# FFN and gate of a four-layer decoder trunk as one piece in a fixed order, fed by one stream of weights

## The chip, the cores and the metric

The kernel runs on one core of a Trainium2 chip. The metric is the device time of one execution in microseconds (us). The engines are called as the profile calls them: PE (TensorE's matmuls; PEld its weight loads), DVE (VectorE), ACT (ScalarE), POOL (GpSimd) and SP (SyncE, which issues all DMAs here).

## The reference, cut to what matters

Four layers; each adds a token mixer, a SwiGLU FFN and a gated embedding to a residual stream `h` of 256 tokens by 1024. The mixers are latent attention (layers 0 and 3), a Conformer convolution (layer 1) and an HGRN2 recurrence (layer 2). All is float32.

```python
for i in range(DEPTH):                       # 4
    u = _rmsnorm(h, norm1_g[i])
    h = h + mixer_i(u)                       # mla, conv, hgrn2, mla
    h = h + _swiglu(_rmsnorm(h, norm2_g[i]), ffn_w_gu[i], ffn_w_down[i])   # 1024 -> 2 x 2816 -> 1024
    gate = jax.nn.sigmoid(_rmsnorm(h, ple_norm_g[i]) @ ple_w_gate[i])      # 1024 -> 1024
    h = h + (p[i] @ ple_w_proj[i]) * gate
return _rmsnorm(h, final_norm_g)
```

## The kernel before, in words

**Matmuls.** The 256 tokens are two tiles of 128 (t = 0, 1). Every float32 operand is split into a high and a low float32r part, and `mm` (lines 219 to 224) makes three matmuls for each product: high x high, high x low, low x high. The token operand is the stationary side; the weights move, 512 columns at a time.

**Weights.** `granule` (168 to 189) loads 512 KB of weights into a buffer `raw` (4 buffers) and splits it: ACT copies the high part (`whi`, 9 buffers, line 182), then DVE subtracts for the low part (`wlo`, 8 buffers, line 183). Only when DVE is done is that `raw` free for the next load. `ktiles` (191) makes granules of two k-tiles of 128 rows by 512 columns; a gate-up granule has two DMAs, the others one. `behind()` orders a split after the instructions in `T.fence`.

**The token side.** `Norm.do(t)` (66 to 89) squares `h` on ACT (line 74, two halves of 512 columns), forms the reciprocal root with eleven small DVE instructions that hang on each other (`rsqrt`, 270 to 294), and transposes 8 blocks of 128 on PE in two groups of four (`split_T`, line 257). Each block leaves PSUM as a high part by ACT (264) and a low part by DVE (265). A `full` norm (before conv and hgrn) first writes `hg` = `h` times the root (line 83, DVE, two halves); the others transpose `h` itself and use the root later. With `defer` (before hgrn) tile 1 is transposed only after the first projection of tile 0 (`finish`, 91).

**FFN** (`ffn`, 359 to 415). Eleven column blocks j of 256. For each (j, t): `up`, 24 matmuls (8 k-tiles x 3) into a bank of gate and up columns; ACT makes Silu (`sg`, 376), DVE the product `ga` (378); two transposes and a split give `aT` (244, 245); `down`, 12 matmuls, adds into four PSUM banks that live through all j. The transposes of a step are put behind the second k-tile of the next `up` (`between`). At the end `residual` (353) adds to `h` and the gate's norm follows. `conv_setup` (layer 0) and `hgrn_setup` (layer 1) are called at j = 2: constants for the mixers of the next layers, a small load `lg`, one transpose of it, an Exp on ACT and about thirty small DVE instructions.

**Gate** (`gate`, 459 to 475, through `linear`, 306). Four groups (t, c) of 24 matmuls, c a half of the 1024 columns; `use` (468 to 473) takes each group with a Tanh on ACT (471) and two DVE instructions (472, 473). After (0, 1) the next norm's tile 0 is done, after (1, 0) the first weights of the next mixer are loaded and split (`pre`), after (1, 1) tile 1.

**What sets the order.** The framework places instructions on each engine by its own estimate of when they are ready, in the order of the program where several are; it may move an instruction of the FFN past another. The engines then run their lists in order. Only the inside of `conv` has an order written by hand: `in_order` (205) chains all instructions of an engine made within it. The 12 small matmuls of `idle` (435) in conv, which have no use but to keep PE at work, go wherever the framework finds a hole.

Of the kernel before, what the change touches and what calls it, by code (L numbers as in the profile page):

```python
# [57 lines left out]
class Norm:  # L58
# [3 lines left out]
    def __init__(self, T, name, i, full=False, defer=False):  # L62
        self.T, self.g, self.full, self.defer = T, T.gains(name, i), full, defer
        self.x, self.r = None, [None] * NT

    def do(self, t):
        T, nc = self.T, self.T.nc
        if self.x is None:
            self.x = T.operand(KD)
        h = T.h[t]  # L70
        ss = T.tmp("ss", [P, 2], 4)
        halves = [slice(c * 512, (c + 1) * 512) for c in range(2)]
        for c, s in enumerate(halves):
            square = nc.scalar.activation(T.tmp("junk", [P, 512], 1, BF16), h[:, s], AF.Square, accum_out=ss[:, c : c + 1])
        if not self.full:
            fence = T.split_T(h, self.x, 0, t, self.g)
        tot = T.tmp("sst", [P, 1], 4)
        nc.vector.tensor_tensor(out=tot, in0=ss[:, 0:1], in1=ss[:, 1:2], op=ALU.add)
        r = self.r[t] = T.rsqrt(tot, 1.0 / D)
        if self.full:  # L80
            hg = T.tmp("hg", [P, D], 1)
            for s in halves:
                last = nc.vector.tensor_scalar(out=hg[:, s], in0=h[:, s], scalar1=r, scalar2=None, op0=ALU.mult)
            if t == NT - 1 and self.defer:
                self.hg = hg
                fence = [square.ins, last.ins]
            else:
                fence = T.split_T(hg, self.x, 0, t, self.g)
        T.fence = fence

    def finish(self, behind):

        with self.T.tc.issue_after(behind):
            self.T.fence = self.T.split_T(self.hg, self.x, 0, NT - 1, self.g)


class Out:


    def __init__(self, T, row):  # L100
        self.T, self.g = T, T.gain(row)

    def do(self, t):
        T, nc = self.T, self.T.nc
        h = T.h[t]
        ss = T.tmp("ss", [P, 2], 4)
        halves = [slice(c * 512, (c + 1) * 512) for c in range(2)]
        for c, s in enumerate(halves):
            nc.scalar.activation(T.tmp("junk", [P, 512], 1, BF16), h[:, s], AF.Square, accum_out=ss[:, c : c + 1])
        tot = T.tmp("sst", [P, 1], 4)  # L110
        nc.vector.tensor_tensor(out=tot, in0=ss[:, 0:1], in1=ss[:, 1:2], op=ALU.add)
        r = T.rsqrt(tot, 1.0 / D)
        y = T.tmp("hg", [P, D], 1)
        for s in halves:
            nc.vector.scalar_tensor_tensor(out=y[:, s], in0=h[:, s], scalar=r, in1=self.g[:, s], op0=ALU.mult, op1=ALU.mult)
            nc.sync.dma_start(T.out[t * P : (t + 1) * P, s], y[:, s])


class Trunk:
# [235 lines left out]

    def ffn_head(self, i):
        return self.ktiles(self.a["ffn_w_gu"][i], [(0, 256), (DFF, 256)])

    def ffn(self, i, norm, done, pre):
        nc = self.nc  # L360
        wgu, wdn = self.a["ffn_w_gu"][i], self.a["ffn_w_down"][i]
        NJ = DFF // 256
        with self.scope(self.nm("ffn")) as pool:
            acc = [[self.acc() for c in range(2)] for t in range(NT)]
            ws, aT = {0: self.head}, {}

            def up(j, t, between=None):
                if t == 0:
                    if j:
                        ws[j] = self.ktiles(wgu, [(j * 256, 256), (DFF + j * 256, 256)])  # L370
                    aT[j] = self.operand(2, "aT", 6, pool)
                r = norm.r[t]
                ps = self.bank("mm", 2)
                self.mms(ps, self.cut(norm.x, t), ws[j], between)
                sg = self.tmp("sg", [P, 256], 2, pool=pool)
                nc.scalar.activation(sg, ps[:, :256], AF.Silu, scale=r)  # L376
                ga = self.tmp("ga", [P, 256], 2, pool=pool)
                nc.vector.scalar_tensor_tensor(out=ga, in0=ps[:, 256:], scalar=r, in1=sg, op0=ALU.mult, op1=ALU.mult)  # L378
                return lambda: self.split_T(ga, aT[j], 0, t)

            wd = {}

            def down(j, t):
                if t == 0:
                    wd[j] = [self.granule([(wdn[(2 * j + k) * P : (2 * j + k + 1) * P], 0)], 1, D) for k in range(2)]
# [6 lines left out]
                if j == NJ - 1:  # L392
                    for c in range(2):
                        self.residual(t, c, acc[t][c])
                    done(t)

            turn = None
            for j in range(NJ):
                if j == 2 and i == 0:
# [4 lines left out]
                if j:  # L404
                    down(j - 1, 1)
                if j == NJ - 1:
                    turn()
                    down(j, 0)
# [796 lines left out]
```

## Time and profile before

| | us |
|---|---|
| median of 3 runs | 1404.83 |
| lowest, highest | 1404.08, 1407.93 |
| the profiled execution's own time | 1409.67 |
| its span, first to last instruction | 1407.9 |

The profiled execution took 1.77 us more than its span, and 4.84 us more than the median of the runs. Times within it count from its first instruction. The mean granted clock is 0.99. Matmul records carry a modelled end, so the distance from one start to the next is read rather than the length of a record. A few matmul records are missing.

### The profile page before, as it was taken

The page shows a single profiled execution, that of the slowest core. Times are in us where ns is not written, and L with a number is a line of the kernel's source. Part 1 is how long each engine was busy: PE and PEld are TensorE (multiplying, and loading weights), DVE is VectorE, ACT ScalarE, POOL GpSimd, SP SyncE. Part 2 cuts the span into 40 slices and gives each one's busy share as a digit, 9 for nine tenths or more (in the row PEclk, how much of TensorE's full clock was granted, in tenths as well). Part 3 has the DMA queues.
Part 4 walks back from the last instruction along what each step waited for, and adds up shares of the span by engine and source line. Part 5 has one row for each costly group of instructions (what it writes and reads, how often), then busy time and mean ns, then how long its engine had stood idle before and what let it go on. Part 6 is the DMA issues. An engine that isn't in the chain of part 4 may idle for free.

```text
span 1407.9 us, 20128 instructions
## 1 busy us (share of the span) xinstructions
PE 1349.1 (96%) x7153; PEld 1100.0 (78%) x7153; DVE 898.1 (64%) x1855; ACT 750.0 (53%) x1353; POOL 14.6 (1%) x51
## 2 busy tenths in 40 slices
PE   6899999999898999999899999999999899999997
PEld 6677788787886888887788887878878777788875
DVE  6866555548787855556777768555568856655546
ACT  6776544436535654445654536444447766544444
POOL 0000000000000000000000000000000000000000
PEclk9999999999999999999999999999999999999999
DMA  6512655553685565554474434655543512766532
GB/s 201 183 61 90 209 182 184 184 169 112 225 241 166 162 211 182 180 179 141 128 224 135 128 91 139 220 179 180 181 159 121 195 60 78 226 191 194 190 109 90
DMA packets 174021, 228.14 MB, mean 162 GB/s; under 512 B 11712, under 2 KB 138848, under 8 KB 173920
## 3 DMA queue, kind: packets, MB, share of 16 engines
q1 hardware_dynamic: 173920, 226.85, 51.1%
q8 instruction: 56, 0.92, 0.3%
q14 instruction: 45, 0.37, 0.1%
HBM read 222.27 MB, written 1.05 MB: 159 GB/s over the span
## 4 chain that ended last, share of the span: by engine, by line
PE 67%; DVE 12%; DMA 9%; ACT 9%; issue 3%; SPq 1%; DVEq 0%; ACTq 0%
PE mm L222 12%; PE mm L224 12%; PE mm L223 12%; PE acc L223 7%; PE acc L224 7%; PE acc L222 7%; DVE wlo L183 4%; ACT whi L182 4%; PE tr L257 3%; DMA raw<-in_ffn_w_down_dram 2%; DVE xT L265 2%; DMA raw<-in_ffn_w_gu_dram 1%; ACT xT L264 1%; DMA raw<-in_ple_w_gate_dram 1%; PE acc L1057 1%
## 5 line engine op out<-in xcount | busy, mean ns | idle before, releaser
L183 DVE TENSOR_TENSOR wlo<-raw,whi 128x1024 fp32r<-128x1024 f32 (+2 forms) x420 | 496.3, 1199 | 169.1 <-ACT whi L182 124.0
L182 ACT ACTIVATE whi<-raw 128x1024 fp32r<-128x1024 f32 (+2 forms) x420 | 428.9, 1041 | 242.0 <-DMA raw<-in_ffn_w_down_dram 87.3
L222 PE MATMUL mm<-whi,xT 128*128 128x512 f32 x816 | 328.8, 403 | 0.0
L223 PE MATMUL mm<-wlo,xT 128*128 128x512 f32 x816 | 320.9, 393 | 1.7 <-DVE wlo L183 1.7
L224 PE MATMUL mm<-whi,xT 128*128 128x512 f32 x816 | 322.0, 395 | 0.0
L224 PEld LDWEIGHTS mm<-whi,xT 128*128 128x128 f32 x816 | 153.5, 188 | 32.5
L223 PEld LDWEIGHTS mm<-wlo,xT 128*128 128x128 f32 x816 | 154.0, 189 | 31.7 <-DVE wlo L183 2.7
L222 PEld LDWEIGHTS mm<-whi,xT 128*128 128x128 f32 x816 | 153.9, 189 | 29.3 <-ACT xT L264 0.4
L223 PE MATMUL acc<-wlo,aT 128*128 128x512 f32 x352 | 138.6, 394 | 0.0
L222 PE MATMUL acc<-whi,aT 128*128 128x512 f32 x352 | 138.5, 394 | 0.0
L224 PE MATMUL acc<-whi,aT 128*128 128x512 f32 x352 | 136.2, 389 | 0.1
L378 DVE SCALAR_TENSOR_TENSOR ga<-mm,rs_y,sg 128x256 f32<-128x256 f32 x88 | 42.3, 480 | 139.8 <-ACT sg L376 139.8
L376 ACT ACTIVATE sg<-mm,rs_y 128x256 f32<-128x256 f32 x88 | 40.9, 465 | 134.6 <-PE mm L224 134.5
L222 PE MATMUL acc<-whi,xT 128*128 128x512 f32 (+2 forms) x272 | 103.4, 385 | 5.4 <-ACT xT L264 4.4
L223 PE MATMUL acc<-wlo,xT 128*128 128x512 f32 (+2 forms) x272 | 104.1, 384 | 2.8 <-DVE wlo L183 2.8
L224 PE MATMUL acc<-whi,xT 128*128 128x512 f32 (+2 forms) x272 | 103.3, 382 | 0.3 <-DVE xT L265 0.3
L264 ACT ACTIVATE xT<-tr,gT 128x128 fp32r<-128x128 f32 x208 | 68.2, 363 | 41.4 <-PE tr L257 21.0
L222 PEld LDWEIGHTS acc<-whi,aT 128*128 128x128 f32 x352 | 66.1, 188 | 16.4 <-ACT aT L244 2.0
L224 PEld LDWEIGHTS acc<-whi,aT 128*128 128x128 f32 x352 | 66.1, 188 | 15.9 <-DVE aT L245 1.2
L223 PEld LDWEIGHTS acc<-wlo,aT 128*128 128x128 f32 x352 | 66.2, 188 | 13.0
L265 DVE SCALAR_TENSOR_TENSOR xT<-tr,gT,xT 128x128 fp32r<-128x128 f32 x208 | 67.0, 345 | 12.1 <-ACT xT L264 9.0
L245 DVE TENSOR_TENSOR aT<-tr,aT 128x256 fp32r<-128x256 f32 x88 | 37.2, 423 | 54.1 <-ACT aT L244 54.1
(266 smaller groups left out, 1759.9 us busy)
## 6 DMA issues: line engine op xcount, KB each, us to landing
raw<-in_ffn_w_gu_dram SPq DMA_DIRECT2D x352, 256.0 KB, 4.4
raw<-in_ffn_w_down_dram SPq DMA_DIRECT2D x88, 512.0 KB, 4.5
raw<-in_ple_w_gate_dram SPq DMA_DIRECT2D x32, 512.0 KB, 4.9
raw<-in_hgrn_w_in_dram SPq DMA_DIRECT2D x64, 256.0 KB, 4.1
raw<-in_mla_w_out_dram SPq DMA_DIRECT2D x16, 512.0 KB, 4.0
raw<-in_conv_w_pw_dram SPq DMA_DIRECT2D x32, 256.0 KB, 4.6
raw<-in_mla_w_in_dram SPq DMA_DIRECT2D x16, 336.0 KB, 3.4
raw<-in_mla_w_uq_dram SPq DMA_DIRECT2D x12, 384.0 KB, 3.8
```

Of the source, the lines that this page charges most:

```text
L182: nc.scalar.activation(hi[:, :used], raw[:, :used], AF.Copy)
L183: nc.vector.tensor_tensor(out=lo[:, :used], in0=raw[:, :used], in1=hi[:, :used].bitcast(F32), op=ALU.subtract)
L222: mm(ps, x[0], w[0], start=start, stop=False)
L223: mm(ps, x[0], w[1], start=False, stop=False)
L224: return mm(ps, x[1], w[0], start=False, stop=stop)
L245: v = self.nc.vector.tensor_tensor(out=lo, in0=src, in1=hi.bitcast(F32), op=ALU.subtract)
L257: nc.tensor.transpose(pt[:, (i - k0) * P : (i - k0 + 1) * P], src[:, i * P : (i + 1) * P], self.ident)
L264: a = nc.scalar.activation(hi, pv[:, i - k0], AF.Copy, scale=g[i])
L265: v = nc.vector.scalar_tensor_tensor(out=lo, in0=pv[:, i - k0], scalar=g[i], in1=hi.bitcast(F32), op0=ALU.mult, op1=ALU.subtract)
L376: nc.scalar.activation(sg, ps[:, :256], AF.Silu, scale=r)
L378: nc.vector.scalar_tensor_tensor(out=ga, in0=ps[:, 256:], scalar=r, in1=sg, op0=ALU.mult, op1=ALU.mult)
L1057: nc.tensor.matmul(ps[:, hh, t], kb[:, hh, tok(t)], right(qf[:, hh, tok(t)]), start=True, stop=True)
```

## The change

`ffn` and `gate` become one function inside `in_order(PE, ACT, DVE, SP)`: the instructions of each of these four engines run as the program lists them. The order is written out: in each step `up` of two k-tiles, the transposes of the step before, weight splits (two `down` granules at t = 0; three granules of the next block at t = 1, the fourth after the Silu), the other six k-tiles, the Silu and product, `down` of the step before. The last block, the gate, the residuals, the two norms around the gate and the next mixer's first splits follow in a written order with three endings (`close`): before conv, hgrn and mla; the fourth, `store`, is the final norm, which took the place of the class `Out`.

All weights of an FFN, its gate and the beginning of the next mixer come from one `Stream`: a list of granules in the order of their use. Four are loaded when the stream is made (in the mixer's `pre`), and each split is followed by the load of the granule four further on. `Norm.do` is cut into `squares`, `root` and `turn`. `hgrn_setup` and `conv_setup` are now called inside the order, behind step (2, 1). The number of matmuls, splits, norms and bytes stays as it was. `lg` is loaded on SP's list where `hgrn_setup` stands in the order.

The core of the diff (mixers take their first weights from the stream instead of from `conv_head` and the like; that is left out):

```diff
+class Stream:
+    AHEAD = 4
+    def __init__(self, items):
+        self.items, self.loaded = list(items), []
+        for _ in range(self.AHEAD):
+            self.load()
+    def load(self):
+        if self.items:
+            later = []
+            self.loaded.append((self.items.pop(0)(later), later))
+    def split(self, n=1):
+        out = []
+        for _ in range(n):
+            x, later = self.loaded.pop(0)
+            for f in later:
+                f()
+            self.load()
+            out.append(x)
+        return out
...
+        items = [row(0), row(1)]
+        for j in range(1, DFF // 256):
+            items += self.granules(wgu, [(j * 256, 256), (DFF + j * 256, 256)])
+            items += [row(2 * j), row(2 * j + 1)]
+        for c in range(2):
+            items += self.granules(wg, [(c * 512, 512)])
+        self.stream = Stream(items + self.mixer_items(i + 1))
+        return head
...
+        with self.scope(self.nm("ffn")) as pool, self.in_order(ENG.PE, ENG.Activation, ENG.DVE, ENG.SP):
...
+            steps = [(j, t) for j in range(NJ) for t in range(NT)]
+            for n, (j, t) in enumerate(steps[:-1]):
+                last = steps[n - 1] if n else None
+                up(j, t, 0, 2)
+                if last:
+                    turn(*last)
+                if t == 0:
+                    wd[j] = w.split(2)
+                elif j + 1 < NJ:
+                    ws[j + 1] = sum(w.split(3), [])
+                up(j, t, 2, KD)
+                act(j, t)
+                if t == 1 and j + 1 < NJ:
+                    ws[j + 1] += w.split(1)[0]
+                if last:
+                    down(*last)
+                if j == 2 and t == 1 and i == 0:
                     self.conv_setup()
-                if j == 2 and i == 1:
+                if j == 2 and t == 1 and i == 1:
                     self.hgrn_setup()
-                turn = up(j, 0, turn)
-                if j:
-                    down(j - 1, 1)
-                if j == NJ - 1:
-                    turn()
-                    down(j, 0)
-                    turn = up(j, 1)
-                    pre()
-                    turn()
-                else:
-                    turn = up(j, 1, turn)
-                    down(j, 0)
-            down(NJ - 1, 1)
-
-
-    def embed_weights(self, i, later=None):
+            j = NJ - 1
+            turn(j, 0)
+            up(j, 1, 0, 2)
+            gate_weights(0, 2)
+            down(j, 0)
+            for c in range(2):
+                self.residual(0, c, acc[0][c])
+            gnorm.squares(0)
+            up(j, 1, 2, 5)
+            gnorm.turn(0, 0)
+            up(j, 1, 5, 6)
+            gnorm.turn(0, 1)
+            up(j, 1, 6, KD)
+            act(j, 1)
+            gate_weights(0, 2)
+            gnorm.root(0)
+            gate(0, 0, 0, 3)
+            turn(j, 1)
+            gate(0, 0, 3, KD)
+            gate_weights(1, 2)
+            use(0, 0)
+            down(j, 1)
+            for c in range(2):
+                self.residual(1, c, acc[1][c])
+            gnorm.squares(1)
+            gate_weights(1, 2)
+            gate(0, 1, 0, 3)
+            gnorm.turn(1, 0)
+            gate(0, 1, 3, 6)
+            gnorm.turn(1, 1)
+            gate(0, 1, 6, KD)
+            gnorm.root(1)
+            use(0, 1)
+            self.close(i, nnorm, gate, use, w)
...
+    def close(self, i, nnorm, gate, use, w):
+        gate(1, 0, 0, KD)
+        if nnorm is None:
+            self.store(gate, use)
+            return
+        kind = (i + 1) % 3
+        nnorm.squares(0)
+        nnorm.root(0)
+        if kind == 1:
+            w.split(1)
+            use(1, 0)
+            self.wp = w.split(1)
+            gate(1, 1, 0, 4)
+            nnorm.turn(0, 0)
+            gate(1, 1, 4, KD)
+            nnorm.turn(0, 1)
+            self.wp += w.split(1)
+        elif kind == 2:
+            use(1, 0)
+            gate(1, 1, 0, 2)
+            nnorm.turn(0, 0)
+            head = w.split(1)[0]
+            gate(1, 1, 2, KD)
+            nnorm.turn(0, 1)
+            head += w.split(1)[0]
+        else:
+            use(1, 0)
+            gate(1, 1, 0, 2)
+            nnorm.turn(0, 0)
+            head = w.split(1)
+            gate(1, 1, 2, KD)
+            nnorm.turn(0, 1)
+            head += w.split(1)
+        use(1, 1)
+        nnorm.squares(1)
+        if kind == 0:
+            nnorm.turn(1, 0)
+            head += w.split(2)
+            nnorm.turn(1, 1)
+            nnorm.root(1)
+            head += w.split(4)
+        else:
+            nnorm.root(1)
+            if kind == 1:
+                head = w.split(2)
+                head = head[0] + head[1]
+                nnorm.turn(1)
+            else:
+                head += w.split(1)[0] + w.split(1)[0]
+        self.head = head
```

`store` runs, after `gate(1, 0)`: the squares of tile 0, its root, scaling and output, `use(1, 0)`, the first square of tile 1, `gate(1, 1)`, `use(1, 1)`, the second square, root, scaling and output of tile 1.

More of the change, by code (lines that the diff above doesn't have):

```diff
@@ L91, in finish @@
     def finish(self, behind):
         with self.T.tc.issue_after(behind):
[L94 to L116, printed above, removed]
+            self.turn(NT - 1)
```

227 lines of the change are left out of this document (135 added, 92 removed).

## The prediction

> **What bounds the kernel now.** I read the page first, for the shares.
>
> ```profile
> span 1407.9 us, 20128 instructions
> PE 1349.1 (96%) x7153; PEld 1100.0 (78%) x7153; DVE 898.1 (64%) x1855; ACT 750.0 (53%) x1353; POOL 14.6 (1%) x51
> ```
>
> PE is the bound over the whole, so a change of order can gain only what PE still waits. Next I cut the span into stretches: from a layer's first FFN matmul to the last matmul of its gate (four rows), then from there to the end of the next mixer's first projections (24 narrow conv matmuls; 48 of hgrn; 96 of mla) or to the end (four rows). Columns: stretch, its length, busy time and count of PE, PEld, DVE, ACT, POOL, granted clock, DMA.
>
> ```profile
> 134.76:351.88 217.12, 214.46 (x972) 172.79 (x970) 126.02 (x206) 107.88 (x168) 2.83 (x9) 1.00 0.55 175
> 474.49:689.20 214.71, 213.08 (x964) 172.63 (x963) 126.33 (x218) 109.84 (x170) 0.00 (x0) 1.00 0.56 178
> 857.15:1073.86 216.71, 213.99 (x966) 172.52 (x965) 131.29 (x212) 112.83 (x174) 0.00 (x0) 1.00 0.57 180
> 1184.31:1398.00 213.69, 211.46 (x955) 171.70 (x953) 124.17 (x199) 105.00 (x160) 0.00 (x0) 1.00 0.54 174
> ...
> 351.88:369.10 17.22, 13.18 (x56) 10.13 (x57) 13.83 (x31) 12.61 (x23) 2.36 (x1) 0.87 0.82 277
> 689.20:706.50 17.30, 14.16 (x58) 10.84 (x57) 14.22 (x30) 12.30 (x21) 0.00 (x0) 0.90 0.51 135
> 1073.86:1091.00 17.14, 16.50 (x109) 15.65 (x108) 13.41 (x54) 12.62 (x32) 0.29 (x1) 1.00 0.45 144
> 1398.00:1407.90 9.90, 0.17 (x1) 0.00 (x0) 4.59 (x15) 1.41 (x3) 0.00 (x0) 0.72 0.14 53
> ```
>
> The four FFN and gate stretches are 862.2 us together, and PE is idle in only 9.2 of them. The pitch of the matmuls gives the rest of what can be lost: from the PE timeline, start to start.
>
> ```profile
> 201.97 0.40 PE L224 MATMUL mm<-whi,xT 128*128 128x512 f32 x1
> 202.20 0.38 PE L257 MATMUL tr<-ident,ga 128*128 128x128 f32 x2
> 202.66 0.40 PE L223 MATMUL mm<-wlo,xT 128*128 128x512 f32 x1
> ...
> 203.13 0.39 PE L222 MATMUL mm<-whi,xT 128*128 128x512 f32 x1
> ...
> 206.32 0.39 PE L224 MATMUL mm<-whi,xT 128*128 128x512 f32 x1
> ...
> 692.74 0.39 PE L222 MATMUL mm<-whi,xT 128*128 128x512 f32 x1
> ...
> 695.23 0.39 PE L224 MATMUL mm<-whi,xT 128*128 128x512 f32 x1
> 698.26 1.14 PE L257 MATMUL tr<-ident,hg 128*128 128x128 f32 x8 [2.65 <-DVE hg L83]
> ...
> 699.97 0.63 PE L223 MATMUL mm<-wlo,xT 128*128 128x512 f32 x1
> ...
> 702.53 0.43 PE L223 MATMUL mm<-wlo,xT 128*128 128x512 f32 x1
> ```
>
> From 203.13 to 206.32 there are 14 steps, from 692.74 to 695.23 eleven: 0.228 and 0.226 us, so 0.227. Two transposes add (202.66 - 201.97) - 2 x 0.227 = 0.236, or 0.118 each. A stretch holds 22 x 36 + 96 = 888 matmuls and 72 transposes (64 in the last): 201.6 + 8.5 = 210.1 us (209.1). So the four lose 862.2 - 839.4 = 22.8 us. That is all the FFN and gate have to give. The waits of PE say to whom:
>
> ```profile
> PE tr L257 <- DVE hg L83: 6.1, 4, 2.6
> PE tr L257 <- DVE ga L378: 3.3, 6, 1.5
> PE acc L223 <- DVE wlo L183: 2.8, 5, 0.7
> PE mm L223 <- DVE wlo L183: 1.7, 3, 0.7
> ```
>
> Every one is DVE. So I looked for what DVE must do around the gate: mean durations between 312 and 372 us, and one reciprocal root alone on DVE.
>
> ```profile
> L183 DVE TENSOR_TENSOR wlo<-raw,whi 128x1024 fp32r<-128x1024 f32 x16 | 18.9, 1219 | 2.9 <-ACT whi L182 2.9
> L182 ACT ACTIVATE whi<-raw 128x1024 fp32r<-128x1024 f32 x16 | 16.1, 1050 | 3.5 <-DMA raw<-in_ple_w_gate_dram 2.5 <-DMA raw<-in_conv_w_pw_dram 1.0
> L74 ACT ACTIVATE junk<-h 128x512 bf16<-128x512 f32 x8 | 5.0, 629 | 5.3 <-DVE h L353 3.1 <-DVE h L473 2.2
> L353 DVE TENSOR_TENSOR h<-acc,h 128x512 f32<-128x512 f32 x4 | 2.7, 687 | 2.0 <-PE acc L224 2.0
> L473 DVE TENSOR_TENSOR h<-h,th 128x512 f32<-128x512 f32 x4 | 2.7, 684 | 0.0
> ...
> 358.35 0.16 DVE L78 TENSOR_TENSOR sst<-ss 128x1 f32<-128x1 f32 x1 [0.17 <-ACT junk L74]
> ...
> 360.25 0.16 DVE L292 SCALAR_TENSOR_TENSOR rs_y<-rs_t,rs_y 128x1 f32<-128x1 f32 x1
> 360.45 0.88 DVE L83 TENSOR_SCALAR hg<-h,rs_y 128x512 f32<-128x512 f32 x2
> ```
>
> A low part takes 18.9/16 = 1.18 us of DVE, a residual or gate addition 0.69, a root alone 2.06 (358.35 to 360.41), `hg` 0.9. A block of a norm's transposes (high by ACT, low by DVE) takes 0.39 in a row of them, since ACT waits for DVE again after each pair:
>
> ```profile
> 362.79 0.62 ACT L264 ACTIVATE xT<-tr,gT 128x128 fp32r<-128x128 f32 x2 [0.49 <-PE tr L257]
> ...
> 365.14 0.37 ACT L264 ACTIVATE xT<-tr,gT 128x128 fp32r<-128x128 f32 x1 [0.16 <-DVE xT L265]
> ```
>
> (six steps in 2.35 us). A group of four is 1.6.
>
> **The change part by part.**
>
> ```profile
> L378 DVE SCALAR_TENSOR_TENSOR ga<-mm,rs_y,sg 128x256 f32<-128x256 f32 x88 | 42.3, 480 | 139.8 <-ACT sg L376 139.8
> L376 ACT ACTIVATE sg<-mm,rs_y 128x256 f32<-128x256 f32 x88 | 40.9, 465 | 134.6 <-PE mm L224 134.5
> ```
>
> *FFN steps.* A step is 36 matmuls and two transposes, 8.4 us, with three splits on average, 3.5 us of DVE and 3.2 of ACT, and Silu and `ga` at 0.5 each. Loads go out about a step before their split. A `ga` is wanted 18 matmuls (4.1 us) after its `up`, 6 (1.4) in the first step, and its chain is 1.2. So the waits for `ga` and for `wlo` into `mm` go, at most 5.0 us of idle, and nothing in the steps is late next.
>
> *The gate block, where `up(10,1)` ends (time 0).* DVE's list in the new order, each end by the sums above: four blocks of the second transposes and `ga` 1.6; two low parts 4.0; root 6.0; `aT` 6.4; two low parts 8.8; the two instructions of `use(0,0)` 10.3 with its halved root; two residuals 11.7. Then ACT: last square with its read-out 12.5, high part 13.5. DVE: low part 14.7. That low part is wanted by k-tile 4 of `gate(0,1)`. PE gets there after 9 + 15 + 12 + 9 + 3 matmuls and 6 transposes, 10.9 + 0.7 = 11.6. So PE loses 3.1 us here, at several points (`aT`, residual, whole weights), because behind one late instruction the fixed order holds all others of its engine: residuals stand behind four splits and a root that nobody wants yet. A wait costs its restart too: from 695.23 to 698.26 are 3.03 us for 2.65 idle and one pitch, 0.15 more; at five points 0.8. That is 3.9 a layer, 15.6 for four, and about 1 more in layer 1, where the transposes before hgrn wait for `hg`: 16.6. Against 22.8 now: -6. But of the 22.8, 9.2 are idle and some 5 restarts and the small matmuls that fill holes; some 8 no row names, and if those stay it is +2. I take -3, nearer to the first, as most small losses stand beside waits. If all the idle time went it would be -9.
>
> *`hgrn_setup`.* Its DMA has been on its way for 45 us when it is wanted. Rows of the `lg` tile and of the DMA issues:
>
> ```profile
> L954 SPq DMA_DIRECT2D lg<-in_hgrn_lb_logits_dram x1: 347/347/347, 461.4 to 461.4; - x1
> L956 PE MATMUL tr<-ident,lg x1: 244/244/244, 506.3 to 506.3; 32*128 32x32 f32 x1
> ...
> DMA to landing us min/median/max: 1.5/1.5/1.5
> ```
>
> In the new order it stands on SP behind a load whose `raw` comes free when DVE has done the fourth split of the step: Silu, high part, low part, 0.5 + 1.05 + 1.22 and lags, 3.1 us after `up(2,1)`; then two issues and its own at 0.35, landing 1.5: 5.7. The transpose of it is next on PE after `down(2,0)`, 12 matmuls, 2.7. Wait 3.0 us. What is queued behind: on PE `up(3,0)`, on ACT the Exp and the splits, on DVE some thirty small ones. They delay `aT` of (2,1), which PE wants 7 us later, so no second wait; POOL, 1% busy, has its part done before. `conv_setup` has two loads and no reader in the FFN: 0. At the rows above, a wait of 2.65 us is followed by a pitch of 0.427 (699.97 to 702.53, six steps), 1.8 us lost until the pitch is back. So 3.0 + 1.8 = 4.8, between 2 and 5. TensorE: Matmul & The Clock Gate of the Trainium skill, in its part on oscillation, has the clock fall only after idle gaps above some 3.4 us; by that this term would be 3.0. The trace shows the fall after 2.65, and I go by the trace.
>
> *The endings.* Here `turn(0,1)` and a split stand ahead of the last Tanh, and everything after it hangs on that. First DVE's lag when the last gate matmul ends. From the end of `gate(0,1)`: transposes' blocks and root 3.9, `use(0,1)` 5.4, square 6.2, root 8.2, `hg` 9.1, embedding input 9.8, `use(1,0)` 11.3, low part 12.5, four blocks 14.0; PE needs 48 matmuls and four transposes, 11.4. DVE lags 2.6 (before hgrn, without the input and with PE itself waiting, 1.0; before mla, without `hg`, 0.8).
> Conv: after the last gate matmul 0.45 transposes, 1.6 blocks, 1.2 low part, 1.4 `use`, 0.8 square, 2.1 root, 0.9 `hg`, 2.4 two low parts, 0.7 first block, and the lag: 13.9 to the first matmul, 5.9 more for the other blocks and the last two low parts: 19.8, and 1.2 at the lower clock: 21.0. Now 17.2: +3.8. The 24 matmuls of the embedding (5.5 us) lie within.
> Hgrn: the third granule's low part comes after 0.45 + 1.6 + 1.2 + 1.4 + 0.8 + 2.1 + 0.9 + 1.2 + 1.0 = 10.6; 12 matmuls 2.7, transposes 0.9, 24 matmuls 5.4, lower clock 1.8: 21.4. Now 17.3: +4.1. Its cover, 24 matmuls for tile 0, is gone with the two granules that are split last.
> Mla: granules are 672 columns, low part 1.18 x 672/1024 = 0.8. The fifth comes after 0.45 + 1.6 + 0.8 + 1.4 + 0.8 + 1.6 + 1.6 + 1.6 + 2.1 + 0.8 + 0.8 = 13.5; the work of the last four of eight granules on both tiles, half of 16.5 - 13 x 0.118, is 7.5: 21.0. Now 17.1: +3.9, and +0.5 if PE finds tile 1's work to fill with.
> The final norm: the chain after the last gate matmul is the same: 0.
>
> Sum: -3 + 4.8 + 3.8 + 4.1 + 3.9 = +13.6 us. On the profiled execution, 1409.67 us for a span of 1407.9, that makes 1423.3; on the median of 1404.83, which is 4.84 us lower, 1418.4.
>
> **The rivals.**
>
> *The order covers.* If DVE's list in the gate block is done by 11.6 instead of 14.7, and the endings cost what they cost now, the 9.2 us of idle time go: 1395.6, faster. It decides where one root and one split (2.06 + 1.18) of DVE's list find room in its pauses, so that nothing stands behind them. For it: DVE is busy 58% of these stretches (507.8 of 862.2). Against it: the written order has the roots in one piece.
>
> *Nothing measurable.* The lists come out close to what the framework made, and gains in the steps (5.0) are given back at `lg` (4.8): 1404.6, with the endings as they are. Against it: the endings are written anew.
>
> *The clock falls in every gate block too.* Then 4 x 1.8 us more: 1425.6. Against it: there each wait is near 1 us.
>
> **How the numbers follow.** The forecast has a chance of 0.51, the first rival 0.30, the second 0.13, the third 0.06. Within 0.3% (4.2 us, about what a measurement of this kernel can tell) is the second: 0.13; faster 0.30; slower 0.57. The range reaches from the first rival to the third, 1395 to 1426. The forecast's own range is 1410 (endings and `lg` at half their price) to 1425.
>
> **What would show it.** In the changed profile: in the FFN steps no wait of PE for `ga`; a wait of about 3 us for the transpose of `lg`; waits for residual and `wlo` near the gate, 3 us a layer; a stretch of some 21 us behind each of three gates, with DVE busy throughout. Wrong it would be if DVE has idle time between `up(10,1)` and the next mixer while PE runs on, or if those stretches stay at 17 us.

## The result, and the profile after

The changed kernel takes 1489.12 us (median of four runs, 1487.12 to 1491.3); the kernel before, on the same chip, 1406.38 (1404.08 to 1412.26). The ratio is 1.058, 95% interval 1.0545 to 1.0619. Slower was forecast, by 13.6 us; it is slower by 83, far outside the range.

The head of the page after, then the same eight stretches as before, with the same columns: four from a layer's first FFN matmul to its last gate matmul, four from there to the end of the mixer's first projections or of the program.

```profile
span 1489.5 us, 19835 instructions
PE 1384.3 (93%) x7153; PEld 1116.1 (75%) x7153; DVE 911.3 (61%) x1855; ACT 739.6 (50%) x1353; POOL 15.9 (1%) x51
```

```profile
136.70:359.50 222.80, 216.81 (x973) 173.87 (x972) 124.64 (x197) 103.03 (x159) 3.16 (x9) 1.00 0.55 172
492.60:724.50 231.90, 220.21 (x962) 176.04 (x961) 129.34 (x226) 104.10 (x163) 0.00 (x0) 0.98 0.52 165
903.60:1131.90 228.30, 219.92 (x961) 176.19 (x959) 128.49 (x203) 105.29 (x164) 0.00 (x0) 0.98 0.54 168
1253.60:1479.70 226.10, 219.15 (x955) 175.52 (x953) 125.82 (x199) 101.97 (x158) 0.00 (x0) 0.98 0.52 167
```

```profile
359.50:388.33 28.83, 17.06 (x61) 12.36 (x60) 20.77 (x41) 16.73 (x32) 3.10 (x1) 0.73 0.46 148
724.50:750.76 26.26, 17.71 (x63) 12.01 (x62) 15.38 (x35) 15.12 (x29) 0.00 (x0) 0.81 0.29 82
1131.90:1157.42 25.52, 20.70 (x116) 17.94 (x115) 17.20 (x47) 15.91 (x40) 0.00 (x0) 0.93 0.41 130
1479.70:1489.50 9.80, 0.00 (x0) 0.00 (x0) 4.62 (x15) 1.53 (x5) 0.00 (x0) 0.62 0.14 54
```

The four FFN and gate stretches are 909.1 us together against 862.2 (+46.9); PE is idle in 33.0 of them, not 9.2. From a layer's last gate matmul to the next layer's first FFN matmul (359.5 to 492.6, 724.5 to 903.6, 1131.9 to 1253.6) it is 433.9 against 401.0: +32.9, of which 29.0 lie in the three stretches of the endings above and the rest in the mixers. The first FFN begins 1.9 us later, and the end is what it was. PE's longest waits are for ScalarE and VectorE; the load of `lg` is one wait of 5.2:

```profile
PE acc L244 <- ACT whi L204: 13.8, 9, 4.1
PE tr L279 <- DVE ga L431: 12.3, 8, 3.1
PE acc L245 <- DVE wlo L205: 7.6, 12, 1.7
...
PE tr L1127 <- DMA lg<-in_hgrn_lb_logits_dram: 5.2, 1, 5.2
```

But both are busy for a smaller share than before. So what did they wait for? The groups of the blocks of `xT` say it. First before, then after (columns: busy and mean, then the engine's idle time just ahead of them and what ended it):

```profile
L264 ACT ACTIVATE xT<-tr,gT 128x128 fp32r<-128x128 f32 x208 | 68.2, 363 | 41.4 <-PE tr L257 21.0 <-DVE xT L265 19.1
L265 DVE SCALAR_TENSOR_TENSOR xT<-tr,gT,xT 128x128 fp32r<-128x128 f32 x208 | 67.0, 345 | 12.1 <-ACT xT L264 9.0
```

```profile
L286 ACT ACTIVATE xT<-tr,gT 128x128 fp32r<-128x128 f32 x208 | 71.5, 365 | 69.9 <-DVE xT L287 56.7 <-PE tr L279 12.7
L287 DVE SCALAR_TENSOR_TENSOR xT<-tr,gT,xT 128x128 fp32r<-128x128 f32 x208 | 69.4, 348 | 56.5 <-ACT xT L286 54.9
```

The blocks last as long as ever, but each engine now waits for the other: ScalarE 56.7 us in place of 19.1, VectorE 54.9 in place of 9.0. One turn of the third layer's gate norm, on ScalarE:

```profile
1115.74 0.37 ACT L286 ACTIVATE xT<-tr,gT 128x128 fp32r<-128x128 f32 x1 [1.49 <-DVE xT L287]
1116.53 0.37 ACT L286 ACTIVATE xT<-tr,gT 128x128 fp32r<-128x128 f32 x1 [0.42 <-DVE xT L287]
1117.31 0.81 ACT L286 ACTIVATE xT<-tr,gT 128x128 fp32r<-128x128 f32 x2 [0.42 <-DVE xT L287]
1118.54 0.37 ACT L286 ACTIVATE xT<-tr,gT 128x128 fp32r<-128x128 f32 x1 [0.42 <-DVE xT L287]
```

A block starts every 0.79 us, each behind VectorE's low part of the block before; only once do two follow at once, where the turn goes over from one PSUM bank to the other. In both traces a block on ScalarE waits on VectorE's semaphore until the low part of the block before it in the same bank is done. Before, the framework had mixed the blocks of a turn's two banks, so that the block just ahead lay in the other bank and a pair of blocks waited 0.16 us (the prediction's rows from 362.79 to 365.14). The change fixes four from one bank, then four from the other, so that the block just ahead lies in the same bank and each block waits 0.42 us. The Trainium skill (PSUM — Partial Sum Buffer, the section on bank collisions) gives the reason: two engines must not touch a bank, in the same partitions, at the same time, reads against reads included, and the compiler's scheduler puts a dependency between them. The waits here agree with it; what happens without them was not tried.

The theory to be tested: this pairing is the largest part of the loss. Its rival: the places of the splits, residuals and Tanh in the fixed lists are.

### The profile page after: what moved, and what is told of

It is laid out like the page before. It is cut to its first block, busy times and chain, and to the rows that moved or that the text cites. A ratio compares the mean times of both kernels' runs of the same rounds, so it can differ in the third digit from the quotient of the medians.

```text
span 1489.5 us, 19835 instructions
## 1 busy us (share of the span) xinstructions
PE 1384.3 (93%) x7153; PEld 1116.1 (75%) x7153; DVE 911.3 (61%) x1855; ACT 739.6 (50%) x1353; POOL 15.9 (1%) x51
## 4 chain that ended last, share of the span: by engine, by line
PE 73%; DVE 12%; ACT 9%; issue 3%; DMA 2%; SPq 0%; ACTq 0%; DVEq 0%
PE mm L244 13%; PE mm L245 13%; PE mm L246 13%; PE acc L245 8%; PE acc L246 8%; PE acc L244 8%; DVE wlo L205 4%; DVE xT L287 3%; ACT whi L204 3%; ACT xT L286 2%; PE tr L279 2%; PE acc L1228 1%; PE acc L849 1%; PE tr L831 1%; DVE rs_t L309 1%
## 5 line engine op out<-in xcount | busy, mean ns | idle before, releaser
L205 DVE TENSOR_TENSOR wlo<-raw,whi 128x1024 fp32r<-128x1024 f32 (+2 forms) x420 | 491.1, 1205 | 105.3 <-ACT whi L204 94.2
L204 ACT ACTIVATE whi<-raw 128x1024 fp32r<-128x1024 f32 (+2 forms) x420 | 417.4, 1036 | 52.3 <-PE mm L246 20.0
L244 PE MATMUL mm<-whi,xT 128*128 128x512 f32 x816 | 335.6, 412 | 4.5 <-ACT whi L204 2.9
L245 PE MATMUL mm<-wlo,xT 128*128 128x512 f32 x816 | 326.9, 401 | 4.5 <-DVE wlo L205 4.5
L246 PE MATMUL mm<-whi,xT 128*128 128x512 f32 x816 | 326.0, 400 | 0.0
L244 PEld LDWEIGHTS mm<-whi,xT 128*128 128x128 f32 x816 | 155.8, 191 | 37.6 <-ACT whi L204 4.3
L246 PEld LDWEIGHTS mm<-whi,xT 128*128 128x128 f32 x816 | 155.5, 191 | 36.0
L266 ACT ACTIVATE aT<-tr 128x256 fp32r<-128x256 f32 x88 | 33.8, 384 | 271.4 <-PE tr L279 271.4
L244 PE MATMUL acc<-whi,xT 128*128 128x512 f32 (+2 forms) x272 | 107.0, 403 | 13.9 <-ACT whi L204 7.3
L245 PE MATMUL acc<-wlo,xT 128*128 128x512 f32 (+2 forms) x272 | 107.6, 398 | 6.5 <-DVE wlo L205 6.5
L246 PE MATMUL acc<-whi,xT 128*128 128x512 f32 (+2 forms) x272 | 106.4, 394 | 0.3 <-DVE xT L287 0.3
L286 ACT ACTIVATE xT<-tr,gT 128x128 fp32r<-128x128 f32 x208 | 71.5, 365 | 69.9 <-DVE xT L287 56.7
L287 DVE SCALAR_TENSOR_TENSOR xT<-tr,gT,xT 128x128 fp32r<-128x128 f32 x208 | 69.4, 348 | 56.5 <-ACT xT L286 54.9
L246 PEld LDWEIGHTS acc<-whi,aT 128*128 128x128 f32 x352 | 66.1, 188 | 17.2 <-DVE aT L267 2.6
```

What stands on the lines that cost most here:

```text
L204: nc.scalar.activation(hi[:, :used], raw[:, :used], AF.Copy)
L205: nc.vector.tensor_tensor(out=lo[:, :used], in0=raw[:, :used], in1=hi[:, :used].bitcast(F32), op=ALU.subtract)
L244: mm(ps, x[0], w[0], start=start, stop=False)
L245: mm(ps, x[0], w[1], start=False, stop=False)
L246: return mm(ps, x[1], w[0], start=False, stop=stop)
L266: a = self.nc.scalar.activation(hi, src, AF.Copy)
```

## The experiments

Unless an interval is given, a time is of one run. The runs were made in groups, each on a chip of its own, with the kernel before beside it: 1407.95 (`e1`, `e2`, `e4`, `e5`), 1411.40 (`e3`, `e6`, `e7`, `e8`), 1406.66 (`e9` to `e12`), 1406.23 (`f1`, `g1` to `g3`) and 1410.69 (`g4`). Most differences below are between groups, and the kernel before itself lay between 1402 and 1412, so differences under some 5 us are read from the profiles.

**The banks, in the kernel after.** `e1_alternate`:

```diff
 def turn(self, t, half=None):
...
+        if half == 1:
+            return
-        T.fence = T.split_T(src[:, k0 * P : k1 * P], self.x, k0, t, self.g[k0:k1])
+        T.fence = T.split_T(src, self.x, 0, t, self.g)
 def split_T(self, src, x, k, t, g=None):
...
+            blocks += [(i, pv[:, i - k0]) for i in range(k0, k1)]
+        if blocks and self.pinned:
+            blocks.sort(key=lambda b: (b[0] % 4, b[0] // 4))
+        for i, pb in blocks:
```

> Edit of the kernel after: each turn of a norm inside the pinned piece turns all eight parts at once, into both transpose banks, and its eight blocks are split in the order A0, B0, A1, B1, ..., instead of four from one bank and then four from the other. Bank theory (a block on ScalarE waits for VectorE's read of the block before it in the same PSUM bank, so a block takes 0.79 us where two banks in turn take 0.39, and ScalarE and VectorE arrive late at everything queued behind): the wait of xT on ScalarE for xT on VectorE falls from 56.7 us to about 20 (19.1 before the change), and the time falls by 30 to 50 us, to about 1440 to 1460. Rival, order theory (what costs is where the weight splits, the tanh and the residuals stand in the fixed lists; the blocks are only what these lists wait beside): the xT wait falls as well, but the time stays within 8 us of 1489.

`e2_bank_order` is the same with `key=lambda b: b[0]`.

> The control to the run before: the same turning of all eight parts at once, but the blocks split bank by bank (A0 to A3, then B0 to B3), as the kernel after has them. Bank theory: nothing of the loss comes back, 1489 within 8 us, and the xT wait stays at 50 to 60 us. Rival (the early transposes are what helps, since PE has them out of its way): the same gain as the run before.

Measured: 1455.12 and 1488.89. On ScalarE, `e1_alternate` (a turn takes the blocks in quick pairs) and the row of its group:

```profile
1097.14 0.62 ACT L292 ACTIVATE xT<-tr,gT 128x128 fp32r<-128x128 f32 x2 [1.23 <-DVE xT L293]
1097.93 0.62 ACT L292 ACTIVATE xT<-tr,gT 128x128 fp32r<-128x128 f32 x2 [0.16 <-DVE xT L293]
1098.72 0.63 ACT L292 ACTIVATE xT<-tr,gT 128x128 fp32r<-128x128 f32 x2 [0.16 <-DVE xT L293]
```

```profile
L292 ACT ACTIVATE xT<-tr,gT 128x128 fp32r<-128x128 f32 x208 | 68.2, 364 | 40.7 <-DVE xT L293 25.8 <-PE tr L282 13.2
```

and of `e2_bank_order`:

```profile
L292 ACT ACTIVATE xT<-tr,gT 128x128 fp32r<-128x128 f32 x208 | 71.0, 365 | 67.6 <-DVE xT L293 54.6 <-PE tr L282 12.6
```

Two blocks every 0.79 us, 0.39 each. ScalarE's wait falls to 25.8 us, not quite to 20. The two kernels differ in nothing but the order of 104 blocks (13 turns inside the piece), and in 33.8 us. The early transposes give nothing. This part is shown: 34 of 83 us. How much of it are the waits themselves, and how much the lower clock behind them, was not taken apart.

**The banks, in the kernel before.** `e5_before_bank_order` holds only the blocks of those turns in bank order (`pin` is set for the gate's norms and the first norms of layers 1 to 3; the deferred turn before hgrn goes by another call, so 13 turns are held and not 14):

```diff
-    def split_T(self, src, x, k, t, g=None):
+    def split_T(self, src, x, k, t, g=None, pin=False):
+        if pin:
+            with self.in_order(ENG.Activation, ENG.DVE):
+                return self.split_T(src, x, k, t, g)
```

> Edit of the kernel before: in the turns of the gate norm and of the next layer's first norm the blocks are held in bank order (A0 to A3, B0 to B3) on ScalarE and VectorE; nothing else is fixed there. Bank theory: this alone slows the kernel before; 14 turns of eight blocks lose up to 8 x 0.39 = 3.1 us each, 44 us in all, of which the framework covers a part with weight splits put between: 1404 plus 12 to 44 us, and the xT wait grows from 19 to over 40 us. Order theory: the framework fills the holes, within 5 us of 1406.

Measured: 1420.61 beside 1407.95, 12.7 slower, at the low end; ScalarE's wait is 32.5 us in 82 places, more than 19.1 but not over 40. The same order costs less in the kernel before, where the framework may put other instructions between the blocks; that this is why was not tested by itself.

**Whose order.** `e4_free_act_dve` and `e6_no_order` free engines in `ffn`:

```diff
-        with self.scope(self.nm("ffn")) as pool, self.in_order(ENG.PE, ENG.Activation, ENG.DVE, ENG.SP):
+        with self.scope(self.nm("ffn")) as pool, self.in_order(ENG.PE, ENG.SP):
```

and, for the second, `with self.scope(self.nm("ffn")) as pool:` alone.

> Edit of the kernel after: only PE and SP keep the fixed order inside the FFN and gate piece; ScalarE and VectorE are ordered by the framework again. Bank theory: the framework mixes the blocks of both banks where it can, but half turns come one bank at a time, so part of the gain of the alternating run, 10 to 40 us, 1450 to 1480. Order theory: the two lists were the loss, so most of it comes back, 1410 to 1440. A third reading (PE's order and the stream of weights are the loss): no gain, 1480 to 1495 or slower.

> Edit of the kernel after: no engine is held in a fixed order inside the FFN and gate piece; the program's text order and the stream of weights stay. With the lists of ScalarE and VectorE given back alone it was 1434.85. If what is left above 1406 is the fixed order of PE and SP: 1405 to 1420. If it is the stream (loads four granules ahead, splits called at fixed places) or the new text order: 1430 or more. The time of one FFN step, 8.46 us in the undisturbed layers before and 8.56 after, goes with whichever it is; if it stays at 8.56, neither the order of PE nor waits set it.

Measured: 1434.85 and 1427.33. Freeing two engines brings back 54 us, more than the bank theory said; so the rival is right beside it. The lists cost at least some 20 us apart from the banks: ScalarE's wait for VectorE's blocks is still 31.0 us in `e4`, so not all of the banks' 34 is in the 54. With nothing held it is still 16 us above the kernel before of the same group, between the two expectations. The median FFN step stayed at 8.56 us in every layer (8.47 before), so the pace of the steps comes neither from the order of PE nor from a list.

**The load of `lg`.** `e3_lg_early`:

```diff
         make_identity(nc, self.ident)
+        self.lg = self.const.tile([DEPTH * 8, P], F32, name="lg")
+        nc.sync.dma_start(self.lg, a["hgrn_lb_logits"].rearrange("d (h k) -> (d h) k", k=P))
...
-            lg = tmp("lg", [DEPTH * 8, P])
-            nc.sync.dma_start(lg, self.a["hgrn_lb_logits"].rearrange("d (h k) -> (d h) k", k=P))
+            lg = self.lg
```

> Edit of the kernel after: the small table lg is loaded at the program's start instead of inside the second layer's FFN, behind the weight loads on SP; its transpose and the rest of hgrn_setup stay where they are. The after trace shows PE waiting 5.2 us for that load and then 3.0 us lost to matmuls at half clock. If the wait is a wait for the load alone: 7 to 9 us faster than 1489, about 1481. Rival (the step would wait next for the exponential's table load or for the weight splits queued behind on ScalarE, which had also stood still): 3 us or less.

Measured: 1482.83, 6.3 less. The second layer's FFN and gate shrink from 231.9 us to 224.0, by 7.9; the whole program's gain is a little under the 7 to 9 expected. PE's other waits in that stretch are as in the kernel after, and none stands in the place of the 5.2 us: the wait was for the load alone.

**The endings.** `e8_endings_free` ends the fixed order ahead of `self.close(...)`; `e11_heads_early` keeps it and moves the splits (here for hgrn; the other two alike):

```diff
             use(1, 0)
+            head = sum(w.split(4), [])
             gate(1, 1, 0, 2)
             nnorm.turn(0, 0)
-            head = w.split(1)[0]
             gate(1, 1, 2, KD)
             nnorm.turn(0, 1)
-            head += w.split(1)[0]
```

> Edit of the kernel after: the fixed order on all four engines ends behind the gate's root and its second tanh; the endings (the last two gate banks, the next norm, the mixer's first weights) are left to the framework. From the last tanh of a layer to the next layer's first silu the kernel after is 5.0, 10.8 and 9.0 us longer than before, 24.8 in all. If the endings' order is what costs there: 15 to 25 us come back, 1464 to 1474. Rival (what the gate block left late is paid there, whoever orders it): under 8 us.

> Edit of the kernel after, all four engines pinned as there: the mixer's first weights are split together, as soon as the gate's third bank is used (four granules for the third and fourth layer's mixer, both rows of the embedding's projection for the second), instead of one or two at a time between the half turns. Theory of late weights (in the third layer the mixer's first split begins 21.9 us behind the last silu before and 32.5 after, of which the late gate block is 8): 8 to 15 us of the 24.8 that lie behind the last tanh come back, 1474 to 1481. Rival (the blocks of xT, now behind four splits on ScalarE, come as much later as the weights come earlier): 1485 to 1493.

Measured: 1470.11 and 1480.40. The endings' order costs 19 us; splitting the weights together, in the same fixed order, brings back 9.

**Three edits together, two engines free.** `e7_free_alt_lg`, the diffs of `e4`, `e1` and `e3`:

> Edit of the kernel after: three edits at once, ScalarE and VectorE ordered by the framework, turns of eight parts with blocks of the two banks in turn, and lg loaded at the start. If the bank waits are what the two lists lost and the framework had not yet all of it back, the parts add: 1434.85 less 7 to 9 for lg less some 5 for the banks, 1418 to 1425. If the framework had already avoided the banks: 1426 to 1429.

Measured: 1421.14, the parts add. ScalarE's wait for VectorE's blocks went from 31.0 us in `e4` to 13.2: half turns, of one bank each, had kept the framework from mixing (31.1 in `e6` too, which has them; 12.6 in `g1` and 13.6 in `e10`, below, which turn all eight).

**Where `xT` lies.** The last loss had no wait to it: matmuls that wait for nothing were slower wherever the new code ran, in whatever order. One thing that all these runs had in common was memory: `squares` asks for its small tiles ahead of `xT` now. `e9_before_xt_moved`:

```diff
     def do(self, t):
...
-        if self.x is None:
-            self.x = T.operand(KD)
         h = T.h[t]
         ss = T.tmp("ss", [P, 2], 4)
...
+        if self.x is None:
+            self.x = T.operand(KD)
         if not self.full:
```

and three pads, `[P, D + N * t]` in place of `[P, D]` for the tiles of `h` (N is 32, 64, 128, for 128, 256 and 512 bytes):

> Edit of the kernel before: only the place of xT in memory. A norm asks for its xT behind the small tiles of its squares, not ahead of them, so all four xT buffers lie 1,152 bytes higher, where the kernel after has them; the work is the same. In the FFN steps the 512-wide matmuls that wait for nothing follow each other at 227 ns (median) in the kernel before and at 231 in the kernel after, whatever engine is held in order. If the place of xT sets that: the median becomes 231 and the time grows by 3 to 8 us. Rival (it comes from the stream of weights or from the instructions themselves): the median stays at 227 and the time within 4 us of 1407.

> The kernel before with 512 bytes left free ahead of xT: xT lies 512 bytes higher than before, nothing else moves ahead of it. In the kernel before xT begins 94,208 bytes behind the first weight buffer, 23 times 4,096; with 1,152 bytes more the matmuls of the FFN steps had a median of 231 ns in place of 227 and the time grew by 8. If any shift from the multiple of 4,096 does that: 231 and 1412 to 1417. If that one place was odd: 227 and within 4 us of 1406.

> The kernel before with 128 bytes left free ahead of xT. If the remainder that xT's place leaves against 512 (a row of a 128x128 operand holds 512 bytes in a partition) or against 256 decides: 231 ns and 1411 to 1417, as with 1,152 bytes. If it is the distance as such, small shifts harmless: 227 ns and within 4 us of 1406.

> The kernel before with 256 bytes left free ahead of xT. If the remainder against 512 decides, this place is another than the old one: 230 ns or more and 1410 to 1417, or a new value. If the remainder against 256 decides, it is the same as the old one: 227 ns and within 4 us of 1406.

Times: 1415.05 (beside 1406.66), 1408.38 (1406.23), 1413.71 and 1407.89 (1410.69). The duration of one FFN matmul, shortest/median/longest in ns, over the same 120 us of the second layer, tells more: before; 1,152 bytes higher; 128; 256; 512.

```profile
L223 PE MATMUL mm<-wlo,xT x112: 389/389/397, 540.9 to 659.9; 128*128 128x512 f32 x112
```

```profile
L223 PE MATMUL mm<-wlo,xT x107: 387/393/404, 542.1 to 659.5; 128*128 128x512 f32 x107
```

```profile
L223 PE MATMUL mm<-wlo,xT x109: 390/393/404, 540.2 to 659.7; 128*128 128x512 f32 x109
```

```profile
L223 PE MATMUL mm<-wlo,xT x111: 387/389/398, 540.7 to 659.4; 128*128 128x512 f32 x111
```

```profile
L223 PE MATMUL mm<-wlo,xT x109: 387/389/398, 541.8 to 659.7; 128*128 128x512 f32 x109
```

From start to start the medians of all 512-wide matmuls there are 227, 231, 233, 227 and 227 ns. 1,152 and 128 leave 128 when divided by 256; 256 and 512 leave nothing. So the remainder of `xT`'s place against 256 bytes sorts all five, and the expectation by 512 fails. The first shift moves `xT` and the squares' small tiles alone: the matmuls with `xT` go from 227 to 232 ns and those with `aT` stay at 229. The pads move all that lies behind them, and with 128 bytes `aT`'s go to 233 too. So it is the place of the stationary operand. Whether its remainder itself counts or its agreement with that of the weights, which never moved, stays open. At 1,152 bytes the mean pitch rises by 2.9 ns (228.7 to 231.6); over 88 steps of 36 matmuls that is 9 us, beside 8.4 measured. The single time at 128 bytes, 3.0 us above its neighbour, would show nothing without the pitch.

**All four causes out.** `e12_pinned_all` (banks, `lg`, weights, place; four engines held), `e10_all_free` (the same, none held), `g1_lists_free` (PE and SP held). The place:

```diff
     def squares(self, t):
         T = self.T
+        if self.x is None:
+            self.x = T.operand(KD)
```

> Edit of the kernel after, all four engines pinned as there: blocks of both banks in turn, lg loaded at the start, the mixer's first weights split together, xT in its old place. From the alternating run's 1455.12: less 7 for lg, 7 for xT's place and 5 to 10 for the weights, 1431 to 1436. If a fixed order of this kind cannot be brought near the framework's own: above 1440. If these were the causes of nearly all: below 1425.

> Edit of the kernel after: no engine held in order; turns of eight parts with the blocks of both banks in turn; lg loaded at the start; the mixer's first weights split as soon as the gate's third bank is used; xT asked for ahead of the squares' tiles, so that it stands as far behind the weights as in the kernel before. From 1427.33 for no order alone: less 6 for lg, some 5 for the banks, 8 for the place of xT (792 matmuls a layer by 2.4 ns), 5 to 10 for the mixers' weights: 1398 to 1405 if the four causes are the whole loss. If xT's place is not what set the 231 ns: 1406 to 1413. If the mixers' starts do not come from the late splits: 1407 to 1415.

> The pinned kernel with the four causes taken out (1434.61), but only PE and SP held in order; ScalarE and VectorE are the framework's. Lists theory (ScalarE's and VectorE's fixed lists are the 36 us that it lies above the same kernel with nothing held, 1398.94): 1400 to 1412. PE theory (PE waits in its own order for what others could have had later): 1420 to 1435.

Measured: 1434.61, 1398.94 and 1412.82. The first two are as summed. Of the 36 us between the first two the lists of ScalarE and VectorE carry 22, the order of PE and SP 14; the third lies just above the bound set for the lists alone. `g2_two_entries` holds all four engines and moves two entries:

```diff
-            gnorm.squares(1)
             gate_weights(1, 2)
+            gnorm.squares(1)
...
-                if t == 0:
+                if t == 0 and n:
                     wd[j] = w.split(2)
...
                 act(j, t)
+                if n == 0:
+                    wd[j] = w.split(2)
```

> The pinned kernel with the four causes taken out (1434.61), all four engines held, and two entries of the lists moved: the last pair of the gate's weights split ahead of the second tile's squares, and in a layer's first step the first two granules of down weights split behind the silu and its product, not ahead of them. In the trace of 1434.61 PE waits 1.03 us in each of the four gates for that pair, and for the first step's product 1.1, 3.3 and 2.5 us in three layers: 4 to 12 us come back, 1423 to 1431, if the lists cost by a few misplaced entries. Rival (each entry moved delays another): within 3 us of 1434.

Measured: 1420.90, 13.7 us less for two lines moved, a little more than the 4 to 12 expected. PE's wait for `ga` goes from 7.3 us in 4 places (`e12`) to 2.1 in 2.

**The version with nothing held, timed again.** `f1_all_free_timed` is `e10_all_free`, run seven times.

> The version with no engine held in order and the four causes taken out (alternate banks, early lg, mixers' weights together, xT in its old place), timed in five rounds, for an interval. By its one look, 1398.94 beside 1406.66, a ratio of 0.9945: 0.992 to 0.997 if that holds; 0.998 to 1.002 if it was chance.

Measured: 1398.95 (median of seven, 1394.67 to 1407.48) against 1406.23 (eleven, 1402.07 to 1409.86): 0.9942, interval 0.9922 to 0.9961. That is 0.6% less, small but clear of 1. Its four FFN and gate stretches, in the profile of `e10_all_free`:

```profile
132.10:346.10 214.00, 212.73 (x964) 172.93 (x963) 127.27 (x205) 109.42 (x167) 2.84 (x9) 1.00 0.57 185
465.90:680.80 214.90, 212.76 (x965) 173.37 (x963) 129.16 (x215) 111.31 (x167) 0.00 (x0) 1.00 0.59 187
847.70:1062.50 214.80, 212.78 (x965) 173.14 (x964) 131.68 (x211) 112.99 (x173) 0.00 (x0) 1.00 0.57 185
1175.80:1387.50 211.70, 211.19 (x955) 171.96 (x953) 124.97 (x199) 105.68 (x160) 0.00 (x0) 1.00 0.55 175
```

They are 855.4 us, 6.8 under the kernel before, with 5.9 of PE idle. So the new text of the FFN and gate, with its stream and the four edits, is a small gain once the framework orders it; which part of it gains was not taken apart.

## Why the prediction was wrong

- *The step that failed: "A group of four is 1.6."* The 0.39 us a block came from a turn of eight whose blocks the framework had mixed from two banks. The text even noted that ScalarE waits again "after each pair", and did not ask what made the pair. Four from one bank take 4 x 0.79 = 3.2 us. That entry stands in every list that was summed. In the third layer's gate block, from PE's, ScalarE's and VectorE's timelines:

```profile
1096.26 0.40 PE L244 MATMUL acc<-whi,xT 128*128 128x512 f32 x1
...
1096.30 0.63 ACT L286 ACTIVATE xT<-tr,gT 128x128 fp32r<-128x128 f32 x2 [0.42 <-DVE xT L287]
...
1098.92 0.37 ACT L286 ACTIVATE xT<-tr,gT 128x128 fp32r<-128x128 f32 x1 [0.42 <-DVE xT L287]
1099.18 0.47 ACT L429 ACTIVATE sg<-mm,rs_y 128x256 f32<-128x256 f32 x1
...
1099.68 0.48 DVE L431 SCALAR_TENSOR_TENSOR ga<-mm,rs_y,sg 128x256 f32<-128x256 f32 x1
...
1100.22 0.44 PE L279 MATMUL tr<-ident,ga 128*128 128x128 f32 x2 [1.70 <-DVE ga L431]
```

  `up(10,1)` ends where the gate's first matmul starts, at 1096.26. Four blocks stand ahead of the Silu, and `ga` ends 3.9 us later, where the list had 1.6 for blocks and `ga` together. The 34 us between `e2` and `e1` are what the order of the blocks was worth.
- *The gate block, 3.9 us a layer.* The list's last low part was put at 14.7 us; in the third layer it ends 18.0 after `up(10,1)`, and 2.3 of the 3.3 us more are there when `ga` ends. PE's idle time in that block is 1.7 (`ga`) and, over the rest, 3.0: 4.7 where 3.1 was summed. What was not in the sum came behind: the clock fell in three of the four gate blocks (the granted clock is 0.95, 0.90 and 0.89 there, and 1.00 in the first layer's), without any wait above 1.7 us. That was the third rival's mechanism, with a chance of 0.06.
- *The steps: "the waits for `ga` go".* They grew, from 3.3 us to 12.3: 6.8 us stand in the layers' first steps, where two granules of down weights stand ahead of the product, and 5.5 in the gates, where it stands behind the blocks. Queued instructions ahead of the chain had been left out of its 1.2 us. The gates' part is gone in `e1`, most of the other in `g2`.
- *The pitch of 0.227.* It was carried over and became 0.231, by a change of memory that no view of a trace shows.
- *`lg`, 4.8.* Right in kind: a wait of 5.2 where 3.0 was summed, and 7.9 us with the lower clock behind it, where 4.8 was.
- *The endings, 11.8.* Right in place and sign, too small in size. The three stretches came to 28.8, 26.3 and 25.5 us where some 21 each was forecast, 29.0 more than before: two groups of blocks each at twice the price, weights late (9 us by `e11`), and the clock (0.73, 0.81 and 0.93 granted against 0.87, 0.90 and 1.00). The sign "with DVE busy throughout" failed: it is busy 20.8, 15.4 and 17.2 us of them. The lists were summed as if VectorE were the bound, and it waited for ScalarE. (The terms written down for conv make 14.15 to the first matmul, not 13.9.)
- *The final norm, 0*: right, 9.8 us against 9.9.
- *"The order covers"* failed for the lists as written. That the kernel with nothing held comes near its time (1398.95 against 1395.6) does not bear it out, since no written order is left there.
- *A reading that entered no sum.* The rows headed "the waits of PE" are of the whole program: of the 6.1 us for `hg` only 1.2 lie in the FFN and gate stretches, the rest in the endings.

The causes overlap, so they don't add to 83. Taken out one after another: 34 for the banks, 20.5 for `lg`, weights and place, 13.7 for two entries; from there to the version with nothing held, 22 more for what is left in the lists and in PE's order. What in the lists costs that was not taken apart further.

## What to carry to other kernels

A duration taken from a row holds for the order that the row was in: before pricing a step that will be moved, ask what let its neighbours overlap, and for two engines on PSUM whether they were in two banks. When several engines are held in a written order, one late instruction is paid by all behind it, and then by the clock; hold as few as the gain needs. And when matmuls that wait for nothing change pace, compare where their operands lie.

## What was not expected of the hardware

The clock fell without a long gap. PE in the third layer's gate, after:

```profile
1110.59 0.66 PE L279 MATMUL tr<-ident,h 128*128 128x128 f32 x4 [0.48 <-DVE h L375]
...
1113.10 0.50 PE L244 MATMUL acc<-whi,xT 128*128 128x512 f32 x1 [1.16 <-ACT whi L204]
1114.36 0.80 PE L245 MATMUL acc<-wlo,xT 128*128 128x512 f32 x1 [0.76 <-DVE wlo L205]
1114.96 0.63 PE L246 MATMUL acc<-whi,xT 128*128 128x512 f32 x1
1115.38 0.63 PE L244 MATMUL acc<-whi,xT 128*128 128x512 f32 x1
...
1119.65 0.63 PE L246 MATMUL acc<-whi,xT 128*128 128x512 f32 x1
1120.08 0.50 PE L244 MATMUL acc<-whi,xT 128*128 128x512 f32 x1
```

Two stretches of this time, with the columns of the stretches above (the granted clock is the third number from the end):

```profile
1110.10:1113.50 3.40, 1.76 (x9) 1.06 (x8) 1.45 (x3) 2.84 (x6) 0.00 (x0) 1.00 0.06 24
1113.50:1120.30 6.80, 6.04 (x17) 4.77 (x17) 4.31 (x9) 3.14 (x9) 0.00 (x0) 0.50 0.36 104
```

The clock fell at 1113.5. Ahead of it lie idle times of 0.48 and 1.16 us, 1.64 of 3.4 us; the third, 0.76, comes behind. From 1114.96 to 1120.08 the matmuls follow at 0.43 us in place of 0.23. The Trainium skill (TensorE: Matmul & The Clock Gate, its part on oscillation) speaks of idle gaps above some 3.4 us; here no gap was longer than 1.16, and the measurement decides. A single idle time of 1.70 us at 1098.5 was not followed by a fall, so length alone does not decide it; what does is not shown. Over the program, 60 of the 512-wide matmuls were followed by the next at 0.40 to 0.46 us (6 before): 11.9 us lost against 1.2.

The other is the place of `xT`: a shift that leaves 128 bytes when divided by 256 put 4 to 6 ns on the median pitch of 227, and no view shows a wait.
